# One level of Strassen's algorithm in the second half's output projection of an attention layer

## The chip, the core and the metric

The kernel runs on one core of a Trainium2 chip. TensorE (PE in the profile) multiplies matrices into the accumulator memory PSUM, VectorE (DVE), ScalarE (ACT) and GpSimd (POOL) do elementwise work, and SyncE (SP) issues the transfers between the chip's main memory and the working memory SBUF. Every engine works through its own queue in order. The metric is the device time of one execution in microseconds.

## The reference, cut

One layer of a decoder: a sliding-window attention with a sink, a gate, and one output projection between two RMS norms. SEQ is 1024, D_MODEL and BRANCH are 2048, all in float32.

```python
def reference(x, g_pre, g_post, w_in_a, w_out_a, sinks_a, ...):
    h = rmsnorm(x, g_pre[0])
    o, z = swa_sink_mixer(h, w_in_a[0], sinks_a[0])     # q, k, v, z = split(h @ w_in)
    y = (o.astype(z.dtype) * jax.nn.silu(z)) @ w_out_a[0]
    return x + rmsnorm(y, g_post[0])
```

What the change concerns is the last product, u @ w_out with u = o * silu(z): 1024 tokens by 2048 by 2048.

## The kernel before

The 1024 tokens are worked in two halves of 512, four blocks of 128 each. A half goes through v and k, then eight quads of heads (the input projection's q and z columns with attention between them, `in_phase`), then the output projection. Attention of the last quad's blocks is still running when the output projection begins; the constants `SPILL`, `TSL_LAST` and `VSL_LAST` place it among the first 13 k steps.

Products are computed to float32 accuracy in three passes: both factors are split in a high part `hi` (rounded by ACT) and a low part `lo` (the rest, subtracted on DVE), and hi·hi, lo·hi and hi·lo are added in PSUM. `passes` names the three pairs; `k` steps of 128 are the contraction.

Weights come through `stream`, a list of granules of 128x512 in the order of use. `next_granule` takes the next, and keeps the splitting `LOOK_W` = 3 granules and the loads `LOOK_DMA` = 5 ahead. In the first half `pump_split` stores each low part to memory (`kept`), and in the second half it is loaded back, so that DVE subtracts no weights there. The activations' parts come through `parts`: `next_part` keeps the splits of u (`u_hi`, `u_lo`, lines 562 and 563) two ahead.

The second half's output projection runs over four chunks of 512 output columns. For chunks 0 to 2, `out_slot` takes one weight granule and one part of u for each of 16 k steps and issues 12 matmuls, three passes for four token blocks, into four PSUM banks; `y_evac` squares and scales them. Chunk 3's weights (`wl_hi`, `wl_lo`) are loaded meanwhile into the room of h1, and chunk 3 is done block by block (line 843): when a block's 48 matmuls are over, its norm is known, and its four pieces are scaled, added to x and stored (lines 850 to 859) while PE works on the next block.

The program's order on each engine is set by the framework's scheduler from the order of the code, except where `keep_in_program_order` pins it.

Of the kernel before, what the change touches and what calls it, by code (L numbers as in the profile page):

```python
# [46 lines left out]
LOOK_DMA = 5  # L47
WARM = 8
# [16 lines left out]
def tile_swa_layer(  # L65
# [93 lines left out]

    stream = []  # L160
    for half in range(2):
# [9 lines left out]
        for c in range(3 if half else 4):  # L171
            for k in range(KC):
                stream.append((src_out(c, k), 1, "out", ("out", c, k)))
                if half and c and k % 2:
                    kl = 8 * (c - 1) + k // 2
                    stream.append((src_out(3, kl), 1, kl, ("out", 3, kl)))
# [3 lines left out]
    wl = []  # L180
# [5 lines left out]
    def pump_dma(limit):  # L186
        while state["dma"] < min(limit, len(stream)):
            i = state["dma"]
            src, nk, kind, key = stream[i]
            raw = gp.tile([P, 512], F32, tag="raw", name="raw")  # L190
            nc.sync.dma_start(raw.rearrange("p (k c) -> p k c", k=nk) if nk > 1 else raw, src)
            lo = None
            if key in kept:
                lo = wl[1][:, kind, :] if isinstance(kind, int) else lo_tile()
                nc.sync.dma_start(lo.bitcast(F32), kept[key])
# [3 lines left out]
    def pump_split(limit):  # L199
        while state["split"] < min(limit, len(stream)):  # L200
            i = state["split"]
            pump_dma(i + 1)
            raw, lo = raws.pop(i)
            kind, key = stream[i][2:]
            if isinstance(kind, int):
                hi = wl[0][:, kind, :]
            else:
                hi = gp.tile([P, 512], F32R, tag="g_hi", name="g_hi", bufs=G_BUFS)
            nc.scalar.copy(hi, raw)  # L209
            if lo is None:  # L210
                lo = lo_tile()
                eng = nc.gpsimd if kind == "in" and key[2] == 1 else nc.vector
                eng.tensor_tensor(lo, raw, hi.bitcast(F32), op=ALU.subtract)  # L213
                kept[key] = dram.tile([P, 512], F32, name=f"lo{i}")
                nc.sync.dma_start(kept[key], lo.bitcast(F32))
# [3 lines left out]
    def next_granule(look_split=LOOK_W, look_dma=LOOK_DMA):  # L219
        while isinstance(stream[state["use"]][2], int):  # L220
            state["use"] += 1
# [10 lines left out]
    def x_transpose(xs, k, h):  # L232
        pt = ps.tile([P, NB, P], F32, tag="o" if k % 4 == 3 else "s", name="pt_x", bufs=O_BUFS if k % 4 == 3 else S_BUFS)
        for b in range(NB):
            nc.tensor.transpose(pt[:, b, :], xs[:, b, :], ident)
        pt = pt.rearrange("p b t -> p (b t)")
        nc.scalar.activation(h[0][:, k, :], pt, AF.Copy, scale=gcol[:, k : k + 1])
        nc.vector.scalar_tensor_tensor(
            h[1][:, k, :], pt, gcol[:, k : k + 1], h[0][:, k, :].bitcast(F32), op0=ALU.mult, op1=ALU.subtract
# [41 lines left out]
    def v_diff(pool, kv):  # L281
        y = pool.tile([P, 2, NB, P], F32R, tag="vy", name="v_y", bufs=1)
        d = pool.tile([P, NB, P], F32, tag="vd", name="v_d", bufs=1)
# [38 lines left out]
    def in_slot(acc, h, g, fresh, done):  # L322
        gr = next_granule()
        for i in range(4):
            k = g * 4 + i
            for j, (w, hh) in enumerate(passes(gr, h)):
# [3 lines left out]
                    rhs=hh[:, k, :],  # L330
# [185 lines left out]
    def in_phase(half, h, u, pool):  # L516
# [3 lines left out]
        for i in range(NQUAD):  # L520
# [3 lines left out]
            if i % 2 == 0:  # L524
                y = {}
                at(s0 + VSL[half] - 3, lambda y=y, kv=i // 2: y.update(t=v_diff(pool, kv)))
# [86 lines left out]
    def v_slot(pvs, h, k, gr):  # L613
        i = k % 2
        for b in range(NB):
            for j, (w, hh) in enumerate(passes(gr, h)):
                mm = nc.tensor.matmul(  # L617
                    pvs[b // 2][:, b % 2, :],
                    lhsT=hh[:, k, b * P : (b + 1) * P],
# [9 lines left out]
    h_hi = hp.tile([P, KC, HALF], F32R, tag="hh", name="h_hi0")  # L629
    h_lo = hp.tile([P, KC, HALF], F32R, tag="hl", name="h_lo0")  # L630
    h0 = (h_hi, h_lo)
# [74 lines left out]
    rrow1 = const.tile([P, HALF], F32, name="rrow1")  # L706
    with tc.tile_pool(name="att0", bufs=1) as att:
# [19 lines left out]
    h1 = (  # L727
        hp.tile([P, KC, HALF], F32R, tag="hh", name="h_hi1"),
        hp.tile([P, KC, HALF], F32R, tag="hl", name="h_lo1"),
    )  # L730
    with tc.tile_pool(name="out0", bufs=1) as op:
# [14 lines left out]
        def chunk_split(k):  # L746
# [3 lines left out]
            nc.scalar.activation(h1[0][:, k, :], xt, AF.Copy, scale=gcol[:, k : k + 1])  # L750
            nc.vector.scalar_tensor_tensor(
                h1[1][:, k, :], xt, gcol[:, k : k + 1], h1[0][:, k, :].bitcast(F32), op0=ALU.mult, op1=ALU.subtract
# [32 lines left out]
    parts += [lambda k=k: (u1[:, k, :], 512) for c in range(3) for k in range(KC)]  # L785
    parts += [lambda b=b, j=j: (u1[:, 4 * j : 4 * j + 4, b * P : (b + 1) * P], P) for b in range(NB) for j in range(4)]
    with tc.tile_pool(name="att1", bufs=1) as att:
# [12 lines left out]
        accs = out_accs(0)  # L800
        for k in range(SPILL):
            run_events(128 + k)
            out_slot(accs, k, k == 0, False)
# [4 lines left out]
    wl += (  # L808
        hp.tile([P, KC, 512], F32R, tag="hh", name="wl_hi"),
        hp.tile([P, KC, 512], F32R, tag="hl", name="wl_lo"),  # L810
    )
    with tc.tile_pool(name="out1", bufs=1) as op:
        junk = op.tile([P, 512], BF16, name="junk2")
        for c in range(3):
            if c:
                accs = out_accs(c)
            gpo = op.tile([P, 512], F32, tag="gpo", name="gpo1", bufs=2)
            broadcast_row(gpo, g_post[:, c * 512 : (c + 1) * 512])
            for k in range(SPILL if c == 0 else 0, KC):
                out_slot(accs, k, k == 0, k == KC - 1)  # L820
                run_events(128 + 16 * c + k)
            for b in range(NB):
                y_evac(accs[b], 1, b, c, yts[b][:, c * 512 : (c + 1) * 512], gpo, junk)
        pump_split(len(stream))
        assert not events, sorted(events)
        gpo = op.tile([P, 512], F32, tag="gpo", name="gpo1", bufs=2)
        broadcast_row(gpo, g_post[:, 3 * 512 : 4 * 512])
        part = op.tile([P, NB], F32, name="part")
        nc.vector.tensor_reduce(part, ssp[:, 1, :, 0:3], axis=AX.X, op=ALU.add)
        nc.vector.tensor_scalar(part, part, 1.0 / D, EPS, op0=ALU.mult, op1=ALU.add)  # L830
        for b in range(NB):
            blk = NB + b
            acc = ps.tile([P, 512], F32, tag="acc", name="acc_l", bufs=4)
            xt = []
            for c in range(4):
                xt.append(op.tile([P, 512], F32, tag="xt1", name="xt1", bufs=4))
                nc.sync.dma_start(xt[c], xf[blk * P : (blk + 1) * P, c * 512 : (c + 1) * 512])
            for k in range(KC):
# [41 lines left out]
```

## Time and profile before

| | |
|---|---|
| median of 3 runs | 1275.54 us (1273.07 to 1280.38) |
| the profiled execution | 1278.27 us, its span 1276.6 us |
| PE busy | 1247.0 us (98%), granted clock 0.992 on average |
| DVE, ACT, POOL busy | 830.6, 783.2, 337.1 us |
| moved by DMA | 274 MB, 215 GB/s on average |
| second half's output projection | first matmul at 1084.9 us, end of the last at 1268.1 us |

Times within the profile are us from the start of the span. Busy time of PE counts matmuls that overlap, so PE's rate is read from the distance of starts. A group's row gives its count, busy time, mean ns of one, and the engine's idle time before its instructions with what ended it.

### The profile page before, as it was taken

To read this page: it belongs to the slowest core of one execution; us is meant where nothing else is said; L and a number is where in the kernel's file an instruction comes from. 1 tells how busy PE (TensorE), PEld (TensorE's weight loads), DVE (VectorE), ACT (ScalarE), POOL (GpSimd) and SP (SyncE) were. 2 spreads that over 40 slices of the span, in tenths; PEclk is the share of its full clock that TensorE was granted. 3 is DMA by queue.
4 is the path that set the end of the run, shared out by engine and by line. 5 is a ranking of instruction groups with operands and counts; after the bars stand their busy time and mean duration, and the time that the engine had idled before them with its cause. 6 is when DMAs were issued, how large, how long until landed. Compare 5 with 4: busy or idle time off the path is not lost.

```text
span 1276.6 us, 20454 instructions
## 1 busy us (share of the span) xinstructions
PE 1247.0 (98%) x5889; PEld 1043.8 (82%) x5889; DVE 830.6 (65%) x2365; ACT 783.2 (61%) x2087; POOL 337.1 (26%) x549
## 2 busy tenths in 40 slices
PE   8989999999999989999999999999999999999997
PEld 8878888888887877888898888888888888877785
DVE  5636767667676688677732278787787777832344
ACT  4526767666666677555533377777767767854531
POOL 1332536536535532000003022242232232200000
PEclk9989999999999999999999999999999999999999
DMA  8556777767676755899886667667767676876625
GB/s 289 157 181 205 224 225 228 221 217 237 215 233 210 232 159 168 230 271 252 253 265 194 190 208 209 210 205 208 213 202 218 191 226 183 290 257 229 226 70 182
DMA packets 302576, 274.03 MB, mean 215 GB/s; under 512 B 51568, under 2 KB 213888, under 8 KB 302464
## 3 DMA queue, kind: packets, MB, share of 16 engines
q1 hardware_dynamic: 302464, 272.73, 70.0%
q8 instruction: 47, 0.77, 0.2%
q14 instruction: 65, 0.53, 0.2%
HBM read 198.21 MB, written 74.45 MB: 214 GB/s over the span
## 4 chain that ended last, share of the span: by engine, by line
PE 54%; DMA 3%; ACT 1%; issue 1%; DVE 1%; POOL 0%; DVEq 0%; POOLq 0%; ACTq 0%; SPq 0%
PE acc_i L318 28%; PE acc_o L318 10%; PE acc_s L318 7%; DMA raw<-in_w_out_a 3%; PE acc_l L843 3%; PE o_ps L447 2%; PE acc_v L617 2%; PE acc_k L318 2%; PE s_ps L318 1%; ACT u_hi L562 1%; ACT g_hi L209 0%; DVE y L855 0%; ACT junk L587 0%; DVE u_lo L563 0%; ACT wl_hi L209 0%
## 5 line engine op out<-in xcount | busy, mean ns | idle before, releaser
L318 PE MATMUL acc_i<-h_hi,g_hi 128*128 128x512 f32 x1024 | 401.3, 392 | 2.0 <-ACT g_hi L209 2.0
L318 PE MATMUL acc_i<-h_hi,g_lo 128*128 128x512 f32 x1024 | 401.0, 392 | 1.7 <-DVE g_lo L213 1.7
L318 PE MATMUL acc_i<-h_lo,g_hi 128*128 128x512 f32 x1024 | 400.7, 391 | 0.0
L209 ACT CAST g_hi<-raw 128x512 fp32r<-128x512 f32 x400 | 245.7, 614 | 123.8 <-PE acc_i L318 49.5
L318 PEld LDWEIGHTS acc_i<-h_hi,g_hi 128*128 128x128 f32 x1024 | 192.8, 188 | 41.2 <-ACT g_hi L209 2.4
L318 PEld LDWEIGHTS acc_i<-h_lo,g_hi 128*128 128x128 f32 x1024 | 193.0, 188 | 40.0
L318 PEld LDWEIGHTS acc_i<-h_hi,g_lo 128*128 128x128 f32 x1024 | 193.0, 189 | 34.0 <-DVE g_lo L213 2.0
L213 DVE TENSOR_TENSOR g_lo<-raw,g_hi 128x512 fp32r<-128x512 f32 x176 | 127.4, 724 | 62.0 <-ACT g_hi L209 60.0
L374 ACT ACTIVATE t<-t,m 128x129 f32<-128x129 f32 x256 | 102.6, 401 | 95.7 <-DVE m L364 93.9
L563 DVE TENSOR_TENSOR u_lo<-u,u_hi 128x512 fp32r<-128x512 f32 x128 | 88.9, 697 | 111.0 <-ACT u_hi L562 104.9
L425 POOL TENSOR_SCALAR_AFFINE_SELECT g<-f 64x512 fp32r<-64x512 f32 x112 | 99.8, 892 | 171.1 <-ACT f L421 135.3
L562 ACT CAST u_hi<-u 128x512 fp32r<-128x512 f32 x128 | 78.9, 618 | 84.9 <-PE acc_o L318 29.0
L405 ACT COPY px<-wt 32x128 f32<-32x128 f32 x324 | 96.3, 297 | 28.6 <-DVE wt L399 25.0
L318 PE MATMUL acc_o<-g_hi,u_hi 128*128 128x512 f32 x256 | 101.9, 398 | 4.6 <-DVE z L510 3.6
L318 PE MATMUL acc_o<-g_lo,u_hi 128*128 128x512 f32 x256 | 101.1, 395 | 0.0
L318 PE MATMUL acc_o<-g_hi,u_lo 128*128 128x512 f32 x256 | 100.5, 398 | 0.1
L364 DVE CUSTOM_DVE_ANT_0 t<-s_ps,t,nsink 128x128 f32<-128x128 f32 x256 | 87.9, 348 | 5.2
L345 POOL COPY t<-nsink 128x4 f32<-128x4 f32 x64 | 12.8, 203 | 277.4 <-DVE w L385 132.8
L144 POOL TENSOR_TENSOR rs_r<-rs_v,mhalf 128x1 f32<-128x1 f32 (+1 forms) x10 | 6.3, 645 | 297.0 <-DVE rs_v L142 297.0
L318 PE MATMUL s_ps<-k_x,q 128*128 128x320 f32 x256 | 76.6, 310 | 3.5 <-POOL q L503 3.5
L362 DVE COPY_PREDICATED s_ps<-mask,s_ps 128x64 f32<-128x64 uint32 x224 | 49.0, 223 | 46.0 <-PE s_ps L318 44.6
L422 DVE TENSOR_TENSOR f<-px,f 128x512 fp32r<-128x512 f32 x64 | 50.7, 793 | 41.6 <-ACT f L421 41.2
(150 smaller groups left out, 2179.3 us busy)
## 6 DMA issues: line engine op xcount, KB each, us to landing
raw<-in_w_in_a SPq DMA_DIRECT2D x288, 256.0 KB, 3.6
lo<-g_lo SPq DMA_DIRECT2D x208, 256.0 KB, 2.7
g_lo<-lo SPq DMA_DIRECT2D x192, 256.0 KB, 3.5
raw<-in_w_out_a SPq DMA_DIRECT2D x128, 256.0 KB, 4.0
pd<-wt SPq DMA_DIRECT2D x28, 256.0 KB, 2.2
px<-pd SPq DMA_DIRECT2D x112, 64.0 KB, 2.2
xp<-in_x SPq DMA_DIRECT2D x16, 256.0 KB, 3.9
xb<-in_x SPq DMA_DIRECT2D x64, 64.0 KB, 4.1
```

The source lines that it names most:

```text
L209: nc.scalar.copy(hi, raw)
L213: eng.tensor_tensor(lo, raw, hi.bitcast(F32), op=ALU.subtract)
L318: ins = nc.tensor.matmul(*args, **kw)
L362: nc.vector.copy_predicated(s3[:, :, P:], mask.unsqueeze(1).broadcast_to([P, 2, QTR]), s3[:, :, 0:QTR])
L364: nc.vector.tensor_tensor_reduce(out=t[:, 0:P], in0=s3[:, 0, QTR:], in1=t[:, 0:P], scale=1.0, scalar=nsink[:, i : i + 1], op0=ALU.add, op1 ...
L374: nc.scalar.activation(t, t, AF.Exp, bias=m, scale=-1.0, accum_out=den)
L405: copy(x[qrows[3 - k], c, :], wt[qrows[c], 3 - k, :])
L422: pin(nc.vector.tensor_tensor(f[:, 1], x, f[:, 0].bitcast(F32), op=ALU.subtract))
L425: nc.gpsimd.affine_select(out=g[dst].rearrange("p a (s i) -> p (a s) i", i=HD), in_=f[HD:P, l].rearrange("p a (s i) -> p (a s) i", i=HD).b ...
L562: nc.scalar.copy(hi_v, src)
L563: nc.vector.tensor_tensor(lo_v, src, hi_v.bitcast(F32), op=ALU.subtract)
L843: nc.tensor.matmul(acc, lhsT=uu[:, i * P : (i + 1) * P], rhs=w[:, k, :], start=k == 0 and j == 0, stop=k == KC - 1 and j == 2,)
```

## The change

The second half's product is cut in halves: tokens in two (256 each), k in two (1024 each), and output columns in pairs of chunks (c and c + 1, for c = 0 and 2). For each pair, seven products of halves take the place of eight (Winograd's form with shared sums). With u's quarters u(t, k) and the weights' quarters v, y, z, x (`w_form`, 8 granules each, loaded by `form_loads` into the room of h1):

- products 1 and 2 take plain weights, 3 the plain quarter z; 7 takes z - y, 6 the sum x + (z - y), 4 takes v less that sum, 5 takes z - x. These sums are made in place, 64 in all, on POOL.
- on the side of u, products 5, 6, 7 and 3 take sums of quarters, made on DVE (`u_part`, `u_last`; lines 854, 858, 860 and 869).
- `FORMS` gives the order of the 28 steps of a pair. A step (`form_step`) takes one part of u (two k of 256 tokens) and two weight granules, and issues 12 matmuls, 6 for each granule, into two PSUM banks; steps are counted by n from 0, and step 28 begins the second pair.
- products are added up afterwards: `s1_copy` and `s5_copy` on ACT, `c11`, `c2` and `c12` on DVE, with the squares on ACT (line 971) and the product by the gain on POOL or DVE (line 972).
- the sums' low parts are subtracted on DVE when used (line 201), as are plain weights whose low part isn't stored any more: the first half now stores low parts of chunk 2 and of the second half of k in chunks 1 and 3 only.
- the last product of the second pair is done for token block 0 and then 1 (`lasts`), 48 matmuls; the four blocks are finished by `finish` (line 1014) around it.

To make room, h is held in halves (`new_h`), `rrow1` is the tile `rrow`, and `v_diff` uses the scratch tile `tmp` in the second half.

```diff
+W_TAGS = (("hlo0", "v"), ("hhi0", "y"), ("hhi1", "z"), ("hlo1", "x"))
+FORMS = [(prod, i) for prod, n in ((1, (0, 4)), (2, (0, 3)), (7, (0, 4)), (4, (0, 3)), (2, (3, 4)), (4, (3, 4)),
+                                   (5, (0, 4)), (6, (0, 4)), (3, (0, 4))) for i in range(*n)]
...
+    def form(c, prod, j):
+        if prod == 1:
+            return src_out(c, j), 1, "out", ("out", c, j)
+        key = {2: ("out", c, 8 + j), 3: ("out", c + 1, 8 + j)}.get(prod)
+        def load():
+            x, y, z, v = (w_form[n][:, j, :] for n in "xyzv")
+            if prod == 7:
+                nc.gpsimd.tensor_tensor(y, z, y, op=ALU.subtract)
+            elif prod == 4:
+                nc.gpsimd.tensor_tensor(v, v, x, op=ALU.subtract)
+            elif prod == 5:
+                nc.gpsimd.tensor_tensor(y, z, x, op=ALU.subtract)
+            if key not in kept:
+                return None
...
+            nc.sync.dma_start(lo.bitcast(F32), kept[key])
+            return lo
+        def split(lo):
+            src = w_form[{7: "y", 5: "y", 2: "v", 4: "v", 6: "x", 3: "z"}[prod]][:, j, :]
...
+            nc.scalar.copy(hi, src)
+            if lo is None:
+                lo = lo_tile()
+                nc.vector.tensor_tensor(lo, src, hi.bitcast(F32), op=ALU.subtract)
+            return hi, lo
...
-                kept[key] = dram.tile([P, 512], F32, name=f"lo{i}")
-                nc.sync.dma_start(kept[key], lo.bitcast(F32))
+                if kind != "out" or key[1] == 2 or key[1] % 2 and key[2] >= 8:
+                    kept[key] = dram.tile([P, 512], F32, name=f"lo{i}")
+                    nc.sync.dma_start(kept[key], lo.bitcast(F32))
...
+    def form_loads(n):
+        def load(name, k, c, jp):
+            for j in (2 * jp, 2 * jp + 1):
+                nc.sync.dma_start(w_form[name][:, j, :], src_out(c, 8 * k + j))
+        c = 2 * (n // 28)
+        n %= 28
+        if n < 4:
+            load("v", 1, c, n)
+        if 2 <= n < 6:
+            load("y", 0, c + 1, n - 2)
+            load("z", 1, c + 1, n - 2)
+        if 6 <= n < 10:
+            load("x", 0, c, n - 6)
+        if 7 <= n < 11:
+            for j in (2 * n - 14, 2 * n - 13):
+                x, y = (w_form[m][:, j, :] for m in "xy")
+                nc.gpsimd.tensor_tensor(x, y, x, op=ALU.add)
...
+    def form_step(n):
+        prod, i = FORMS[n % 28]
...
+        u = next_part()
+        for j in range(2):
+            gr = next_granule()
+            for b in range(2):
+                for q, (w, uu) in enumerate(passes(gr, u)):
+                    c0 = j * 2 * P + b * P
+                    ins = nc.tensor.matmul(
+                        accs[b], lhsT=uu[:, c0 : c0 + P], rhs=w,
+                        start=prod != 3 and i + j + q == 0, stop=i == 3 and j == 1 and q == 2, skip_group_check=True,
+                    )
...
+        def c2(c):
+            for b in range(2):
+                nc.vector.tensor_tensor(s1[:, b, :], s1[:, b, :], bank["c"][b], op=ALU.add)
+                nc.vector.tensor_tensor(mid[:, b, :], s1[:, b, :], bank["a"][b], op=ALU.add)
+            for b in range(2):
+                ct = sum_tile()
+                nc.vector.tensor_tensor(ct, mid[:, b, :], bank["d"][b], op=ALU.add)
+                y_take(ct, 2 + b, c, nc.gpsimd)
...
+        def c12(b, c):
+            ct = sum_tile()
+            nc.vector.tensor_tensor(ct, s1[:, b, :], bank["b"][b], op=ALU.add)
+            y_take(ct, b, c + 1, nc.vector)
...
+        lasts = [next_granule() for _ in range(8)]
+        for b in range(2):
...
+            if b == 0:
+                part_sum(slice(2, 4))
+                finish(2, xt2)
+                xt3 = x_load(3, xt_tiles())
+                finish(3, xt3)
+            c12(b, 2)
+            finish(b, xt1 if b else xt0)
```

What this does to the order of the engines is shown at three places. On DVE, after the last attention block, in the first chunk of the output projection before:

```order
L463 TENSOR_TENSOR u_8188<-s_o,z 128x128 x2
L563 TENSOR_TENSOR u_lo<-u_8188,u_hi 128x512 x4
L588 TENSOR_TENSOR y_13579<-acc_o,gpo_13588 128x512 x2
L588 TENSOR_TENSOR y_13580<-acc_o,gpo_13588 128x512
L563 TENSOR_TENSOR u_lo<-u_8188,u_hi 128x512
```

and, on DVE, around products 2, 4 and 5 of the first pair now (w_v, w_y are weight sums, u_sum the sums of u, c_t an output sum):

```order
L515 TENSOR_TENSOR u_8127<-s_o,z 128x128 x2
L201 TENSOR_TENSOR g_lo<-w_v,g_hi 128x512
L858 TENSOR_TENSOR u_sum<-u_8127 128x512 x4
L615 TENSOR_TENSOR u_lo<-u_8127,u_hi 128x512
L201 TENSOR_TENSOR g_lo<-w_v,g_hi 128x512 x2
L615 TENSOR_TENSOR u_lo<-u_sum,u_hi 128x512
L977 TENSOR_TENSOR c_t<-s_8128,acc_f 128x512
L860 TENSOR_TENSOR u_sum<-u_sum,u_8127 128x512
```

Where a step had one u_lo, it now has one u_lo, up to two g_lo and often a sum. On POOL, at the end of attention, before (g are attention's masked weights, px its transposed pieces, rs_r the norm's scale):

```order
L405 COPY px<-wt 32x128 x3
L425 AFFINE_SELECT g<-f 64x512 x2
L405 COPY px<-wt 32x128 x3
L425 AFFINE_SELECT g<-f 64x512 x2
L144 TENSOR_TENSOR rs_r<-rs_v,mhalf 128x1 x4
```

and on POOL now, from the middle of the first pair's weight sums:

```order
L177 TENSOR_TENSOR w_v<-w_v,w_x 128x512
L179 TENSOR_TENSOR w_y<-w_z,w_x 128x512 x3
L477 AFFINE_SELECT g<-f 64x512
L177 TENSOR_TENSOR w_v<-w_v,w_x 128x512
L179 TENSOR_TENSOR w_y<-w_z,w_x 128x512
L177 TENSOR_TENSOR w_v<-w_v,w_x 128x512
L477 AFFINE_SELECT g<-f 64x512
```

Attention's last POOL work stands between weight sums, and each sum waits for what it reads and overwrites. Last, the end of DVE's queue before, where block 3 alone is left (acc_l is the last matmul's bank):

```order
L563 TENSOR_TENSOR u_lo<-u_8188,u_hi 128x512
L142 TENSOR_SCALAR rs_v<-ssp,part 128x1
L852 TENSOR_TENSOR y_13581<-acc_l,gpo_14434 128x512
L146 SCALAR_TENSOR_TENSOR rs_w<-rs_r 128x1
L147 TENSOR_TENSOR rs_w<-rs_w,rs_v 128x1
L148 SCALAR_TENSOR_TENSOR r_114<-rs_w,rs_r 128x1
L855 SCALAR_TENSOR_TENSOR y_13581<-y_13581,r_114,xt_14713 128x512
```

and on DVE now, from the sum of the last bank (the row L998) on:

```order
L998 TENSOR_TENSOR c_t<-s_8128,acc_f 128x512
L145 TENSOR_SCALAR rs_v<-ssp,part 128x1 x3
L972 TENSOR_TENSOR y_13618<-c_t,gpo_14128 128x512
L145 TENSOR_SCALAR rs_v<-ssp,part 128x1
L149 SCALAR_TENSOR_TENSOR rs_w<-rs_r 128x1 x2
L150 TENSOR_TENSOR rs_w<-rs_w,rs_v 128x1 x2
L151 SCALAR_TENSOR_TENSOR r_114<-rs_w,rs_r 128x1 x2
L149 SCALAR_TENSOR_TENSOR rs_w<-rs_r 128x1
L1014 SCALAR_TENSOR_TENSOR y_13619<-y_13619,r_114,xt_14539 128x512
L1014 SCALAR_TENSOR_TENSOR y_13619<-y_13619,r_114,xt_14540 128x512
```

All sixteen operations of line 1014, those of the blocks that were complete earlier too, now stand behind the sum of the last bank.

More of the change, by code (lines that the diff above doesn't have):

```diff
@@ L202, in pump_split @@
             pump_dma(i + 1)
-            raw, lo = raws.pop(i)
[L204 to L208, printed above, removed]
+            kind, key = stream[i][2:]
+            if kind == "form":
+                splits[i] = stream[i][1](raws.pop(i))
+                state["split"] += 1
+                continue
+            raw, lo = raws.pop(i)
+            hi = gp.tile([P, 512], F32R, tag="g_hi", name="g_hi", bufs=G_BUFS)
             nc.scalar.copy(hi, raw)
```

226 lines of the change are left out of this document (156 added, 70 removed).

## The prediction

> **What bounds the kernel now.** I read the engine lines of the page first, then the whole kernel cut into the stretches of its last stage, then that stage's groups and waits, and last the final microseconds in order of time.
>
> ```profile
> PE 1247.0 (98%) x5889; PEld 1043.8 (82%) x5889; DVE 830.6 (65%) x2365; ACT 783.2 (61%) x2087; POOL 337.1 (26%) x549
> ```
>
> PE bounds the kernel as a whole. What this change is worth must be read from the stage that it rewrites: the second half's output projection, from its first matmul at 1084.9 us to its last one's end at 1268.1 us, and the tail behind it.
>
> ```profile
> 1084.89 0.39 PE L318 MATMUL acc_o<-g_hi,u_hi 128*128 128x512 f32 x1
> ...
> 1262.28 0.39 PE L843 MATMUL acc_l<-wl_hi,u_lo 128*128 128x512 f32 x1
> ...
> 1267.71 0.39 PE L843 MATMUL acc_l<-wl_hi,u_lo 128*128 128x512 f32 x1
> ```
>
> Start to start counts, since matmuls overlap. Between the last two rows lie 24 intervals: 5.43 / 24 = 0.226 us a matmul. The stage's 768 matmuls are 173.8 us at that rate and the stage is 183.2 us long; attention's last matmuls and small gaps make the other 9. So PE is the limit here too, and the other engines have room:
>
> ```profile
> 1084.90:1126.00 41.10, 41.10 (x197) 34.55 (x196) 30.46 (x95) 31.90 (x85) 8.43 (x16) 1.00 0.82 279
> 1126.00:1268.10 142.10, 140.38 (x606) 111.99 (x604) 53.62 (x91) 62.12 (x126) 1.65 (x3) 1.00 0.58 193
> ...
> DVE u_lo L563 <- ACT u_hi L562: 77.1, 41, 6.3
> ```
>
> Columns are PE, weight loads, DVE, ACT, POOL, granted clock, DMA share, GB/s. While attention's last blocks run (first row) DVE is 74% busy and ACT 78%. After that DVE is at 38% and POOL is empty: DVE waits 77 us in total for ACT's high parts, with little to do. That idle room is what the change spends.
>
> **The removal.** 12 matmuls make one step, and 52 steps plus 48 matmuls in the end are 672, against 768. 96 x 0.226 = 21.7 us less of PE, which is the largest gain possible.
>
> **What is added to DVE and POOL.** Before, a weight tile served 12 matmuls and its low part came ready from memory. Now a tile of weights or of weight sums serves 6, and 72 tiles have the low part subtracted on DVE again, besides 5 plain ones. The prices come from the groups of operations of this stage (the third row, POOL's, from those of the whole kernel); columns are the count, busy us and mean ns, then idle time before:
>
> ```profile
> L563 DVE TENSOR_TENSOR u_lo<-u,u_hi 128x512 fp32r<-128x512 f32 x61 | 42.3, 697 | 80.9 <-ACT u_hi L562 77.1 <-PE acc_o L318 3.6
> L588 DVE TENSOR_TENSOR y<-acc_o,gpo 128x512 f32<-128x512 f32 x8 | 5.5, 691 | 4.8 <-DMA xt<-in_x 4.1 <-ACT junk L587 0.6
> L213 POOL TENSOR_TENSOR g_lo<-raw,g_hi 128x512 fp32r<-128x512 f32 x32 | 41.5, 1298 | 29.9 <-ACT g_hi L209 14.4 <-DMA raw<-in_w_in_a 12.2 <-DMA lo<-g_lo 2.0
> L209 ACT CAST g_hi<-raw 128x512 fp32r<-128x512 f32 x45 | 27.7, 617 | 1.8 <-PE acc_o L318 1.8
> ...
> 1084.90:1126.00 41.10, 8.41 (x12) 1.00 0.82 279
> ...
> L209 ACT CAST g_hi<-raw 128x512 fp32r<-128x512 f32 x14 | 8.6, 616 | 1.8 <-PE acc_o L318 1.8
> L562 ACT CAST u_hi<-u 128x512 fp32r<-128x512 f32 x13 | 7.9, 615 | 2.4 <-DVE u L463 1.3 <-PE acc_o L318 0.9
> ```
>
> A full-width DVE operation (128x512) is 0.69 us, one on POOL with two inputs 1.29 to 1.30. The last three rows are of 1084.9 to 1126 alone: the u_lo work and ACT's casts in it. So attention's own work in this stage is 30.5 - 8.4 = 22 us on DVE, and 31.9 - 8.6 - 7.9 = 15 us on ACT. Now stage by stage, PE against DVE, counted in the changed order.
>
> A, steps 0 to 23 of the first column pair (all products but the third). PE: 288 x 0.226 = 65, and 5 for attention's matmuls: 70 us. DVE: 45 weight splits, 22 splits of u, 17 sums of u: 84 x 0.69 = 58; two sums from PSUM 1.4; attention 22: 81 us. DVE alone is 11 us longer than PE, and a lookahead of three weight tiles (4 us of PE) can't carry that. So in A DVE sets the pace, even if nothing disturbs it. ACT (45 + 22 casts of 0.62, 15 of attention, 4 of copies and squares) is 61 us and stays under it.
>
> B, steps 24 to 34, whose low parts come from memory. PE: 132 x 0.226 = 30 us; DVE: 26 full-width operations, 18 us. The SP queue issues some 39 transfers of 0.26 MB there; at the 319 GB/s of the row below these are 32 us.
>
> ```profile
> 1084.90:1112.00 27.10, 27.10 (x133) 22.83 (x132) 23.68 (x79) 22.50 (x63) 5.40 (x12) 1.00 0.93 319
> ```
>
> C, steps 35 to 51. PE: 204 x 0.226 = 46 us. DVE: 32 weight splits, 19 of u, sums worth 11, 2 from PSUM: 64 x 0.69 = 44 us. Level.
>
> D, the last 48 matmuls: 11 us.
>
> **POOL against DVE.** 64 weight sums go to POOL, with 10 products by the gain: 34 in A, some 20 in B, some 18 in C. POOL is no bound by itself (34 x 1.29 = 44 us in A), but look at one collision, DVE and POOL in order of time:
>
> ```profile
> 317.26 0.89 DVE L513 SCALAR_TENSOR_TENSOR z<-th,z 128x512 f32<-128x512 f32 x1
> 318.07 0.28 DVE L363 SCALAR_TENSOR_TENSOR t<-distb,s_ps 128x128 f32<-128x128 f32 x1
> 318.27 1.58 DVE L213 TENSOR_TENSOR g_lo<-raw,g_hi 128x512 fp32r<-128x512 f32 x1
> ...
> 317.69 1.62 POOL L284 TENSOR_TENSOR v_d<-v_n 128x512 f32<-128x512 f32 x1
> ...
> 89.06 0.69 DVE L213 TENSOR_TENSOR g_lo<-raw,g_hi 128x512 fp32r<-128x512 f32 x1 [4.73 <-ACT g_hi L209]
> ```
>
> A split that takes 0.69 us alone took 1.58 us: it ended 0.54 us after POOL's operation had ended (319.31), as if it had stood still before. POOL's was itself 0.33 us longer than its 1.29, behind the DVE operation before. The one with an input in PSUM (L363) kept its pace. In the Trainium skill, "SBUF — State Buffer", section "Who interferes with whom", this is a lock: a DVE instruction with two SBUF inputs and a GpSimd instruction that reads SBUF exclude each other for their whole length. The trace agrees (0.69 against 1.58 us), and the rule speaks against this change, since splits and sums of u and the weight sums are all of that kind; by it with 1.29 us lost for each of the 34, A alone would be some 125 us.
>
> The price of one POOL operation to a DVE that is the bound lies between 0 (it falls beside work from PSUM, or in a pause) and 1.15 us (1.29 less the 0.14 that overlapped at the end). I take the row's own loss, 1.58 - 0.69 = 0.89, times the share of DVE's time that has two SBUF inputs: in A (58 + about 8 of attention's 22) / 81 = 0.8, so 0.7 us each; in C nearly all, 0.86. A: 81 + 34 x 0.7 = 105 us. B: 18 + 20 x 0.7 = 32, beside PE's 30 and the transfers' 32: 32 us. C: 44 + 18 x 0.86 = 60, less the 4 of lookahead: 56 us. D: 11. The sum is 204 us against 183.2: 21 us longer. Bounds: with 0 it is 81 + 30 + 46 + 11 = 168 (15 shorter); with 1.15 it is 120 + 34 + 65 + 11 = 230 (47 longer).
>
> **The tail.** Before, three of the four token blocks are finished and stored while PE works on the next; only the last stands behind the last matmul:
>
> ```profile
> 1268.20 0.60 ACT L850 ACTIVATE junk<-acc_l 128x512 bf16<-128x512 f32 x1 [7.82 <-PE acc_l L843]
> 1269.05 0.68 DVE L852 TENSOR_TENSOR y<-acc_l,gpo 128x512 f32<-128x512 f32 x1
> 1270.38 2.74 DVE L855 SCALAR_TENSOR_TENSOR y<-y,r,xt 128x512 f32<-128x512 f32 x4
> ...
> xt<-in_x SPq DMA_DIRECT2D x16, 256.0 KB, 4.6
> out<-y SPq DMA_DIRECT2D x16, 256.0 KB, 3.9
> ```
>
> That is 8.5 us, to the span's end at 1276.6. In the changed order all 16 final operations stand on DVE behind the sum c_t that waits for the last matmul: c_t and a product (1.4), the scales (some 16 small ones of 0.16 to 0.21, 2.8), 16 x 0.685 = 11.0, half a microsecond for block 3's x, whose buffers are block 2's, and 3.9 for the last store: about 20 us. The 20 transfers from the first store on need 16 us at 319 GB/s and end no earlier. Tail: +11.5 us, nothing covers it, and I know of no row that could make it less than +9 or more than +14.
>
> Sum: +21 + 11.5 = +32. The profiled execution took 1278.27 us, 1.7 more than its span and 2.7 more than the median of the runs, 1275.54; a difference carries over, so I forecast 1275.5 + 32.5 = 1308 us.
>
> Costed at nothing: the first half stores 32 low parts less, but PE didn't wait there; the scratch tile that the value difference now shares with tanh is read out before ACT's tanh comes up; the row of scales reuses a tile whose readers are done; the weight loads at the start (8 + 32 transfers) wait for h1's buffers and then take 33 us, under A's 105. If A came out at PE's 70, these and POOL's sums would be late next.
>
> **The rivals.** First, PE stays the bound: DVE catches up by running ahead and POOL's sums fall beside work from PSUM. Then the stage is 152 + 5 = 157 us, the tail 20, and the time 1275.5 - 26 + 11.5 = 1261. For it: the 77 us that DVE idles today. Against it: A needs 81 us of DVE in 70, and the idle is after attention's end, not there; it decides below about 74 us in A. Chance 0.08.
>
> Second, DVE paces A but the collisions cost almost nothing, since POOL's operations find gaps: 168 + 20, so 1275.5 - 15 + 11.5 = 1272, no measurable change (0.5%, 6.4 us, is what a measurement can tell here). For it: many of today's collisions are short, as DVE comes late in POOL's operation:
>
> ```profile
> 160.52 0.99 DVE L213 TENSOR_TENSOR g_lo<-raw,g_hi 128x512 fp32r<-128x512 f32 x1 [0.39 <-ACT g_hi L209]
> ...
> 159.67 1.30 POOL L213 TENSOR_TENSOR g_lo<-raw,g_hi 128x512 fp32r<-128x512 f32 x1 [1.29 <-ACT g_hi L209]
> ```
>
> Here 0.30 us were lost. Against it: that was an engine with pauses (POOL is 26% busy on the page); in A, POOL would be over 40% busy, and a DVE without pauses meets each of its operations. Chance 0.16.
>
> Third, worse: PE, which now waits in every step, loses its clock.
>
> ```profile
> 500.00:505.00 5.00, 2.83 (x12) 1.88 (x10) 4.14 (x8) 4.24 (x11) 0.74 (x1) 1.00 0.46 127
> 505.00:510.00 5.00, 4.26 (x12) 3.38 (x13) 2.09 (x6) 1.15 (x3) 1.05 (x1) 0.51 0.61 206
> ```
>
> After a stretch in which PE was busy 2.8 of 5 us the clock was granted at half. A step is then 5.4 us and not 2.7, more than the 4.4 us that DVE needs in A; if half of the 41 steps of A and C ran so, 20 x about 1.5 = 30 us come on top: 1338. In the Trainium skill, "TensorE: Matmul & The Clock Gate", Part 1, halving needs an idle window of about 3.4 us. A's waits, some 1.7 us a step, would be too short, if spread. Chance 0.12.
>
> That the change removes no matmuls is excluded: its order holds 96 fewer of this stage.
>
> **How the numbers follow.** The forecast has 0.64: 1308, in its own range 1284 (half of the 0.7) to 1336 (the full 1.15 with the tail). The range 1268 to 1338 takes in the second rival and part of the third, and leaves out the first. Faster by over 0.5%: the first rival and a quarter of the second, 0.12; within 0.5%: the rest of the second, 0.12; slower: 0.76.
>
> **What the profile would show.** Right: DVE over 90% busy in steps 0 to 23 and again near the end, PE gaps there released by DVE's g_lo; g_lo's mean above 0.9 us; POOL's w_y, w_x and w_v sums above 1.29; over 15 us from last matmul to end, with 16 final operations of 0.69 in a row. Wrong: g_lo at 0.70 while POOL is busy (second rival), or PE without gaps until the last product (first); a granted clock below 0.9 in the stage speaks for the third.

## The result and the profile after

The changed kernel takes 1329.08 us (median of 4 runs, 1324.74 to 1334.54), the kernel before, run beside it, 1274.3 us (1272.56 to 1280.38). The ratio is 1.0423, with a 95% interval of 1.0367 to 1.0479: slower, by some 55 us. The forecast was 1308 us, in a range up to 1338.

Below, stages A to D and the tail are those of the prediction. Their ends are counted in the trace from the stage's 672 matmuls, 12 to a step. First the stretches of the changed kernel: A, B, C, D, tail. Columns are PE, weight loads, DVE, ACT, POOL, granted clock, DMA share, GB/s.

```profile
1083.10:1199.00 115.90, 85.62 (x322) 65.64 (x321) 108.35 (x172) 61.00 (x136) 59.95 (x50) 0.81 0.44 153
1199.00:1234.30 35.30, 32.50 (x134) 25.68 (x133) 31.90 (x27) 23.33 (x47) 32.06 (x20) 0.95 0.71 253
1234.30:1294.90 60.60, 49.47 (x206) 37.40 (x205) 53.73 (x61) 33.37 (x62) 30.33 (x19) 1.00 0.21 72
1294.90:1305.90 11.00, 11.00 (x49) 8.79 (x47) 8.56 (x12) 4.15 (x10) 3.38 (x2) 1.00 0.09 34
1305.90:1329.70 23.80, 0.01 (x1) 0.00 (x0) 15.33 (x39) 1.45 (x4) 2.72 (x4) 0.56 0.63 220
```

The stage is 222.8 us long where it was 183.2, the tail 23.8 where it was 8.5: 54.9 us in all. It began 1.8 us earlier, which leaves the 53.1 us between the two spans (1329.7 and 1276.6). In A, DVE is busy 108 of 116 us: it sets the pace, and PE, whose busy time there still holds overlaps, doesn't. PE's largest wait in the stage is for DVE's splits of the weights (us in total, times, longest):

```profile
PE acc_f L918 <- DVE g_lo L201: 22.9, 14, 5.4
```

The loss isn't spread evenly. Here are two short stretches (step 7, and steps 35 to 39), and between them one without POOL's work (steps 16 to 23); same columns:

```profile
1117.40:1140.00 22.60, 7.59 (x20) 4.96 (x19) 22.50 (x30) 5.80 (x14) 22.29 (x16) 0.58 0.00 0
...
1175.20:1199.20 24.00, 23.51 (x97) 19.01 (x96) 21.33 (x34) 14.89 (x26) 0.28 (x1) 0.93 0.65 212
...
1234.20:1260.80 26.60, 16.08 (x60) 10.38 (x59) 26.60 (x18) 8.50 (x15) 24.61 (x15) 1.00 0.03 10
```

In the first and the last, DVE and POOL are both busy all the time and PE stands. In the last, 18 DVE operations take 26.6 us, 1.48 each. In the middle one POOL is empty, 34 DVE operations take 21.3 us, and all of its eight steps but the first take PE's own 2.72 us. The groups of the stage show the same by tiles (count, busy us, mean ns of one, idle before):

```profile
L201 DVE TENSOR_TENSOR g_lo<-w_y,g_hi 128x512 fp32r<-128x512 f32 x32 | 37.0, 1167 | 0.1
L615 DVE TENSOR_TENSOR u_lo<-u,u_hi 128x512 fp32r<-128x512 f32 x21 | 29.0, 1396 | 1.3 <-ACT u_hi L614 1.3
L201 DVE TENSOR_TENSOR g_lo<-w_x,g_hi 128x512 fp32r<-128x512 f32 x16 | 10.7, 686 | 0.8 <-ACT g_hi L198 0.8
L437 DVE TENSOR_TENSOR w<-t,rec 128x192 f32<-128x192 f32 (+2 forms) x9 | 8.1, 925 | 0.0
L457 DVE COPY px<-wt 32x128 f32<-32x128 f32 x12 | 7.2, 598 | 0.2
L515 DVE TENSOR_TENSOR u<-s_o,z 128x128 f32<-128x128 f32 x8 | 6.0, 787 | 0.1
...
L179 POOL TENSOR_TENSOR w_y<-w_z,w_x 128x512 f32<-128x512 f32 x16 | 26.5, 1677 | 4.5 <-DVE g_lo L201 4.3
```

The split of w_x, when POOL has nothing to do, is 0.686 us; the same operation on w_y, beside POOL's sums, is 1.167 us. POOL's last sums take 1.68 us instead of 1.29 to 1.30. The last three DVE rows are attention's own work. In order of time the two engines take turns (start, length):

```profile
1125.53 1.31 POOL L177 TENSOR_TENSOR w_v<-w_v,w_x 128x512 f32<-128x512 f32 x1
1125.64 1.75 DVE L201 TENSOR_TENSOR g_lo<-w_y,g_hi 128x512 fp32r<-128x512 f32 x1
1126.81 1.72 POOL L179 TENSOR_TENSOR w_y<-w_z,w_x 128x512 f32<-128x512 f32 x1
```

The split ends 0.55 us after POOL's first sum, and POOL's second 1.14 us after the split.

The tail, PE's last matmul first and then DVE in order of time, and one row of the chain of waits (the second fence):

```profile
1305.52 0.39 PE L1046 MATMUL acc_f<-w_hi,u_lo 128*128 128x512 f32 x1
...
1303.85 1.78 DVE L972 TENSOR_TENSOR y<-c_t,gpo 128x512 f32<-128x512 f32 x1
1305.55 0.68 DVE L998 TENSOR_TENSOR c_t<-s,acc_f 128x512 f32<-128x512 f32 x1
...
1307.49 0.67 DVE L998 TENSOR_TENSOR c_t<-s,acc_f 128x512 f32<-128x512 f32 x1
...
1319.12 0.75 DVE L1014 SCALAR_TENSOR_TENSOR y<-y,r,xt 128x512 f32<-128x512 f32 x1 [1.94 <-DMA xt<-in_x]
1319.79 2.73 DVE L1014 SCALAR_TENSOR_TENSOR y<-y,r,w_x 128x512 f32<-128x512 f32 x4
```
```profile
1313.30 5.80 DMA xt<-in_x
```

The last matmul ends at 1305.9, but the sum that needs it starts at 1307.49: DVE was late, behind products that had met POOL's (1.78 us instead of 0.68). Then DVE stands 1.94 us for block 3's x, whose transfer is 5.80 us of the chain.

### The profile page after: what moved, and what is told of

Same layout as the page of the kernel before. It is cut to its first block, busy times and chain, and to the rows that moved or that the text cites. A ratio compares the mean times of both kernels' runs of the same rounds, so it can differ in the third digit from the quotient of the medians.

```text
span 1329.7 us, 20452 instructions
## 1 busy us (share of the span) xinstructions
PE 1243.7 (94%) x5793; PEld 1034.3 (78%) x5793; DVE 962.1 (72%) x2483; ACT 811.0 (61%) x2135; POOL 454.3 (34%) x623
## 5 line engine op out<-in xcount | busy, mean ns | idle before, releaser
L259 ACT CAST g_hi<-raw 128x512 fp32r<-128x512 f32 x368 | 225.6, 614 | 115.3 <-PE acc_i L370 43.3
L263 DVE TENSOR_TENSOR g_lo<-raw,g_hi 128x512 fp32r<-128x512 f32 x184 | 132.4, 719 | 61.6 <-ACT g_hi L259 60.1
L457 ACT COPY px<-wt 32x128 f32<-32x128 f32 x324 | 96.3, 297 | 36.6 <-DVE wt L451 33.1
L918 PE MATMUL acc_f<-g_lo,u_hi 128*128 128x512 f32 x208 | 88.2, 427 | 27.8 <-DVE g_lo L201 22.9
L615 DVE TENSOR_TENSOR u_lo<-u,u_hi 128x512 fp32r<-128x512 f32 x88 | 75.3, 860 | 37.3 <-ACT u_hi L614 35.1
L614 ACT CAST u_hi<-u 128x512 fp32r<-128x512 f32 x88 | 54.4, 618 | 72.2 <-PE acc_s L370 33.7
L918 PE MATMUL acc_f<-g_hi,u_lo 128*128 128x512 f32 x208 | 85.9, 415 | 1.9 <-DVE u_lo L615 1.9
L918 PE MATMUL acc_f<-g_hi,u_hi 128*128 128x512 f32 x208 | 74.2, 417 | 6.2 <-ACT g_hi L259 3.8
L918 PEld LDWEIGHTS acc_f<-g_lo,u_hi 128*128 128x128 f32 x208 | 42.0, 202 | 45.1 <-DVE g_lo L201 31.3
L415 DVE SCALAR_TENSOR_TENSOR t<-distb,s_ps 128x128 f32<-128x128 f32 x256 | 71.4, 284 | 5.6
```

What stands on the lines that cost most here:

```text
L415: nc.vector.scalar_tensor_tensor(t[:, 0:P], distb, 2.0 ** -i, s3[:, 1, QTR:], op0=ALU.mult, op1=ALU.add)
L457: copy(x[qrows[3 - k], c, :], wt[qrows[c], 3 - k, :])
L614: nc.scalar.copy(hi_v, src)
L615: nc.vector.tensor_tensor(lo_v, src, hi_v.bitcast(F32), op=ALU.subtract)
L918: ins = nc.tensor.matmul(accs[b], lhsT=uu[:, c0 : c0 + P], rhs=w, start=prod != 3 and i + j + q == 0, stop=i == 3 and j == 1 and q == 2, s ...
```

## Experiments

The kernels ran in four groups besides the first pair, each with the kernel before on the same chip (its medians were 1270.57, 1271.35, 1273.56 and 1273.51 us). Ratios are to that. The stage's start in the profiled executions lay between 1076.0 and 1084.4 us; so stage lengths are compared rather than spans. A kernel whose sums are left out, or replaced by writes or copies, no longer computes the layer; it is there for its time alone.

| kernel | median us | ratio, 95% interval | A | B | C | tail |
|---|---|---|---|---|---|---|
| as changed | 1329.08 | 1.0423, 1.0367 to 1.0479 | 115.9 | 35.3 | 60.6 | 23.8 |
| no sums | 1277.65 | 1.0058, 1.0037 to 1.0079 | 82.6 | 32.0 | 47.4 | 23.0 |
| three writes for each sum | 1292.61 | 1.0176, 1.0152 to 1.0201 | 97.9 | 31.6 | 47.4 | 23.3 |
| the same, px copies on ACT | 1292.89 | 1.0152, 1.0121 to 1.0183 | 94.6 | 31.6 | 47.4 | 23.3 |
| one write for each sum | 1285.16 | 1.0099, 1.0070 to 1.0127 | 87.6 | 31.7 | 47.4 | 23.1 |
| one copy for each sum | 1296.13 | 1.0197, 1.0181 to 1.0212 | 93.8 | 30.8 | 54.1 | 23.6 |
| sums on DVE | 1311.56 | 1.0308, 1.0277 to 1.0339 | 105.0 | 35.1 | 51.0 | 23.6 |
| 16 more low parts kept | 1317.54 | 1.0369, 1.0344 to 1.0395 | 107.0 | 34.8 | 60.5 | 23.9 |
| no sums, low parts kept | 1273.76 | 1.0018, 1.0006 to 1.0031 | 79.0 | 31.7 | 47.4 | 23.9 |
| sums on DVE, low parts kept, tail mended | 1296.67 | 1.0211, 1.0189 to 1.0234 | 98.4 | 36.6 | 51.0 | 18.8 |
| no sums, low parts kept, tail mended | 1271.36 | 0.9983, 0.9966 to 1.0001 | 79.2 | 32.0 | 47.4 | 18.9 |

D was 11.0 us in every one.

**Without the sums.**

```diff
-                nc.gpsimd.tensor_tensor(y, z, y, op=ALU.subtract)
+                pass
...  the same for v - x, z - x and x + y
```

> Leaves out all 64 weight sums on POOL (the products then use plain weight tiles); splits, casts, matmuls, loads and the tail stay as they are. Theory (POOL's two-input sums and DVE's two-input operations exclude each other, and DVE paces the stage): g_lo back to about 0.70 us, steps 0 to 23 in 81 to 88 us instead of 116.1, steps 35 to 51 in 46 to 48 instead of 60.6, 24 to 34 in 31 instead of 35; 47 to 54 us less, 1275 to 1282 us. Rival 1 (the 40 loads at the start set the pace of steps 0 to 23): these steps stay above 105 us, about 1315. Rival 2 (PE's halved clock is a cause of its own and stays while PE waits for DVE at all): 20 to 30 us of the gain are missing, 1300 to 1310, with some 40 us at half clock left.

Measured: ratio 1.0058, A 82.6, B 32.0, C 47.4. The theory's numbers hold and both rivals fall. The stretches A and C of this kernel, and four of its groups:

```profile
1078.20:1160.80 82.60, 75.21 (x321) 60.84 (x320) 78.21 (x172) 60.25 (x136) 13.48 (x18) 0.94 0.61 214
...
1192.80:1240.20 47.40, 46.79 (x205) 38.10 (x204) 36.12 (x58) 33.64 (x62) 2.95 (x2) 1.00 0.29 98
```
```profile
L201 DVE TENSOR_TENSOR g_lo<-w_y,g_hi 128x512 fp32r<-128x512 f32 x32 | 22.7, 722 | 0.5 <-ACT g_hi L198 0.5
...
L437 DVE TENSOR_TENSOR w<-t,rec 128x192 f32<-128x192 f32 (+2 forms) x9 | 2.7, 325 | 0.0
L457 DVE COPY px<-wt 32x128 f32<-32x128 f32 x12 | 2.6, 220 | 0.2
L515 DVE TENSOR_TENSOR u<-s_o,z 128x128 f32<-128x128 f32 x8 | 2.0, 285 | 0.0
```

DVE's count of operations is the same in A (172), its busy time 30 us less. And yet this kernel, with 96 matmuls less and no sums to make, is still not faster than before: A stays near DVE's own 78 us, and the tail costs 14.5 us more than before.

**Writes in place of the sums.** Which part of POOL's work blocks DVE?

```diff
-                nc.gpsimd.tensor_tensor(y, z, y, op=ALU.subtract)
+                [nc.gpsimd.memset(y, 0.01) for _ in range(3)]
...  the same for v, y and x
```

> Each of the 64 weight sums on POOL is replaced by three writes of a constant to the same tile (no reading of SBUF), at some 0.5 us each, so POOL stays busy about 1.6 us for each as in the changed kernel, and the splits still wait for POOL's tile. Theory (it is POOL's reading beside DVE's two inputs that blocks): g_lo stays at about 0.70 us and the time is that of the kernel without sums plus at most 6 us, 1275 to 1288. Rival (POOL's tiles come late, or any POOL work on SBUF blocks DVE): g_lo above 1.0 us or long waits for POOL, 1315 to 1330.

Measured: 1292.61 us, between the two expectations, ratio 1.0176. C is as without sums, 47.4 us, with POOL at work; A is 97.9. Groups of this kernel:

```profile
L201 DVE TENSOR_TENSOR g_lo<-w_y,g_hi 128x512 fp32r<-128x512 f32 x32 | 22.3, 704 | 0.6 <-ACT g_hi L198 0.6
L457 DVE COPY px<-wt 32x128 f32<-32x128 f32 x12 | 17.1, 1427 | 0.2
...
L177 POOL MEMSET w_v<- 128x512 f32 x48 | 24.0, 524 | 15.3 <-ACT g_hi L198 14.2 <-DVE g_lo L201 0.7
```

The splits are back at 0.70 us, so it is the reading on POOL that holds up a two-input DVE operation, and writing doesn't. All 13 us that C lost are that. In the Trainium skill, "SBUF — State Buffer", section "Who interferes with whom", this is stated so: a DVE instruction with two SBUF inputs contends with a GpSimd instruction that reads SBUF, not with one that only writes; the trace agrees (1.167 against 0.704 us). But in A 15 us are left over no sums, and one DVE row grew far more than any other: the px copies (17.1 us against 2.6).

> The kernel that writes constants on POOL in place of the sums, with the attention's px copies (32x128, one SBUF input, four of each sixteen on DVE) moved from DVE to ACT in the second half. Theory (in the kernel with constants, steps 0 to 23 took 97.7 us and not 82 because DVE's px copies stood behind whole runs of POOL's writes: 17.1 us for 12 copies, 2.6 without POOL's work): steps 0 to 23 in 82 to 87 us, ratio to the kernel before 1.006 to 1.010. Rival (the 16 us are POOL's lateness with its tiles): no change, ratio 1.015 to 1.020.

```diff
-  copy = {"A": nc.scalar.copy, "P": nc.gpsimd.tensor_copy, "D": nc.vector.tensor_copy}[MOVES[n]]
+  copy = {"A": nc.scalar.copy, "P": nc.gpsimd.tensor_copy, "D": nc.scalar.copy if half else nc.vector.tensor_copy}[MOVES[n]]
```

Measured: A 94.6, ratio 1.0152, in an interval that overlaps that of the kernel it was made from. The theory fell: with the copies gone from DVE its busy time in A drops from 92 to 78 us, and A by 3. The copies now stand in ACT's queue, though, and PE waits for ACT's high parts, so this run doesn't show what A would be if they cost nothing anywhere:

```profile
PE acc_f L918 <- ACT g_hi L259: 5.7, 3, 5.2
PE acc_f L918 <- ACT g_hi L198: 4.8, 3, 4.1
```

So POOL's own time was tried, with `range(1)` in place of `range(3)`.

> As the kernel with three writes of a constant in place of each weight sum, with one write each: POOL is busy some 0.5 us for a sum's tile instead of 1.56, the waits between DMA, POOL, ACT and DVE are the same. Theory (with three writes, POOL's own length sets steps 0 to 23, 95 to 98 us: 34 tiles x 1.56 = 53 us beside attention's POOL work, in a window of some 50 us): with a third of it they fall to 82 to 86 us, ratio to the kernel before 1.005 to 1.009. Rival (the chain of waits through POOL costs this by itself, however short POOL's work): steps 0 to 23 stay above 92 us, ratio 1.013 or more.

Measured: A 87.6, ratio 1.0099. Between the two again: of the 15.3 us, 10.3 go when POOL's 1.56 us become 0.52, and 5.0 stay. The px copies on DVE shrink in the same run, from 17.1 us to 6.6 (12 of 0.55 us), so the two aren't separated here. That A fell by only 3 us when they left DVE speaks for POOL's length as the larger part. What the other 5 us are wasn't settled; the px copies, still 4 us above the 2.6 without the sums, may be part of it.

**A copy in place of each sum.**

```diff
-                nc.gpsimd.tensor_tensor(y, z, y, op=ALU.subtract)
+                nc.gpsimd.tensor_copy(y, z)
...  the same for v (from x), y (from z) and x (from y)
```

> Each of the 64 weight sums on POOL is replaced by a copy of one of its two inputs to the same tile (POOL reads one SBUF tile and writes one), some 1.1 us each. Theory (whatever reads SBUF on POOL excludes DVE's two-input operations): splits beside it are long again, g_lo of w_y above 1.0 us, 1305 to 1320, close to the changed kernel. Rival (only POOL's two-input operations exclude them; the kernel with writes alone showed that writing doesn't): g_lo at 0.70 us, 1278 to 1293.

Measured: 1296.13 us, between the two, ratio 1.0197. One collision and two groups:

```profile
1119.66 1.07 POOL L179 COPY w_y<-w_z 128x512 f32<-128x512 f32 x1
1120.18 1.09 DVE L201 TENSOR_TENSOR g_lo<-w_y,g_hi 128x512 fp32r<-128x512 f32 x1
1120.68 1.07 POOL L177 COPY w_v<-w_x 128x512 f32<-128x512 f32 x1
```
```profile
L201 DVE TENSOR_TENSOR g_lo<-w_y,g_hi 128x512 fp32r<-128x512 f32 x32 | 27.6, 877 | 0.7 <-ACT g_hi L198 0.7
...
L896 POOL COPY w_x<-w_y 128x512 f32<-128x512 f32 x16 | 11.2, 726 | 0.1
```

The split again ends 0.54 us after POOL's operation, as it does beside a sum. A copy that reads holds a split up in the same way. What was wrong is the size: a copy takes 0.73 us and not the 1.1 that I had put, so each takes less from DVE.

**The sums on DVE.**

```diff
-                nc.gpsimd.tensor_tensor(y, z, y, op=ALU.subtract)
+                nc.vector.tensor_tensor(y, z, y, op=ALU.subtract)
...  the same for v - x, z - x and x + y
```

> The 64 weight sums are computed on DVE instead of POOL; everything else is the same. Theory (full exclusion: a sum on POOL costs DVE 0.9 to 1.2 us, on DVE itself 0.69): steps 0 to 23 take 81 + 34 x 0.69 = 105 us instead of 116, steps 35 to 51 about 52 to 55 instead of 60.6; 15 to 23 us less, 1306 to 1314. Rival 1 (a sum on POOL costs DVE no more than 0.7, the price of the prediction): no change, 1325 to 1332. Rival 2 (the sums, in DVE's queue, hold up splits behind them while they wait for loads): over 1335.

Measured: A 105.0, C 51.0, and B unchanged at 35.1: the stage is 20.6 us shorter, the ratio 1.0308, 1.1 points below the changed kernel's. The theory's A came out, 105, though only 32 of the 34 operations counted there are sums (two are products by the gain, which stay on POOL): from the 82.6 measured without sums, 32 x 0.69 more are 104.7. C is a little below the expected 52 to 55, and neither rival came. A sum that the engine in need does itself costs A (105.0 - 82.6) / 32 = 0.70 us; one that another engine does "for free" costs it (115.9 - 82.6) / 32 = 1.04.

**More low parts from memory.**

```diff
-                if kind != "out" or key[1] == 2 or key[1] % 2 and key[2] >= 8:
+                if kind != "out" or key[1] % 2 == 0 or key[2] >= 8:
```

> The first half stores the low parts of 16 more weight tiles (products 1 and 2 of the first column pair), and the stage loads them instead of subtracting them again: 16 splits less on DVE in steps 0 to 23, 16 transfers of 0.26 MB more there. Theory (DVE paces these steps): 16 x 0.69 to 16 x 1.4 = 11 to 22 us less, steps 0 to 23 in 94 to 105 us, 1307 to 1318. Rival (the steps lost time lies in the POOL sums window, steps 3 to 15, or in the loads, not in products 1 and 2): under 5 us less, 1324 to 1330.

Measured: A 107.0, C unchanged at 60.5; the stage is 9.5 us shorter, a little less than the theory's low end of 11. The ratio is 1.0369, and its interval overlaps that of the changed kernel, so the gain is read from the stage.

> The kernel without the 64 weight sums, with the low parts of the first pair's products 1 and 2 also kept in memory, so 16 splits less in steps 0 to 23. Theory (what was left in these steps without the sums, 82 us against PE's 70, is DVE's own work): 82 - 16 x 0.69 = 71 us, PE the bound; stage 173 - 11 = 162, tail 23 as before it: 8 to 11 us less than without sums, a ratio to the kernel before of 0.997 to 1.000. Rival (loads at the start or ACT's casts set those 82 us; 16 more transfers come on top): no change, ratio 1.004 to 1.010.

Measured: A 79.0 and not 71, ratio 1.0018, between the two expectations. Most of A's gain didn't come, which speaks for the rival. A in three stretches (steps 0 to 2, 3 to 7, and 8 to 23), and a wait:

```profile
1080.40:1089.80 9.40, 9.40 (x46) 7.77 (x46) 8.11 (x29) 8.18 (x24) 1.49 (x4) 1.00 1.02 373
1089.80:1109.90 20.10, 18.17 (x78) 12.80 (x77) 17.47 (x47) 16.46 (x43) 3.56 (x7) 1.00 1.04 378
1109.90:1159.40 49.50, 45.49 (x201) 36.59 (x200) 47.89 (x84) 35.26 (x71) 6.83 (x7) 1.00 0.57 193
```
```profile
PE acc_f L918 <- DMA g_lo<-lo: 1.7, 6, 0.4
```

Through step 7 the DMA engines are full (share above 1, 373 to 378 GB/s). In steps 3 to 7 PE meets low parts that are just landing, and a step takes about 4 us. After that DVE is busy 47.9 of 49.5 us. So the loads seem to take over at the start, and DVE stays the limit behind it; no run separates the two.

**The best complete version, and the bound.** In the tail, block 3's x is loaded early, into tiles that are free by then, and the last pair's products go to DVE:

```diff
-                xt3 = x_load(3, xt_tiles())
...
         lasts = [next_granule() for _ in range(8)]
+        xt3 = x_load(3, [w_form["z"][:, c, :] for c in range(4)])
...
-                y_take(ct, 2 + b, c, nc.gpsimd)
+                y_take(ct, 2 + b, c, nc.vector if c else nc.gpsimd)
```

> The best complete version that the parts add up to: the sums on DVE, the 16 low parts kept, and in the tail block 3's x loaded early into the free tiles w_z instead of into block 2's, with the last pair's products by the gain on DVE. Steps 0 to 23: 105 - 16 x 0.69 = 94 us; the rest of the stage as with the sums on DVE (97 us), so 191; tail 23.6 - 1.9 (DVE's wait for x) - 1.2 to 1.7 (collisions with POOL's products) = 20 to 20.5. Ratio to the kernel before 1.018 to 1.022. Rival (tail bound by the stores and not by DVE): tail stays above 22.5, ratio above 1.021. Neither theory has it faster than before.

Measured: ratio 1.0211, tail 18.8 us, better than the 20 expected; A 98.4, above the 94, which wasn't followed further. That the ratio is the expected one is in part chance, since these two misses have opposite signs. Its tail in order of time: no wait is left in DVE's row of final operations.

```profile
1276.85 2.73 DVE L1014 SCALAR_TENSOR_TENSOR y<-y,r,xt 128x512 f32<-128x512 f32 x4
...
1279.92 2.74 DVE L1014 SCALAR_TENSOR_TENSOR y<-y,r,w_z 128x512 f32<-128x512 f32 x4
...
1282.76 5.39 DVE L1014 SCALAR_TENSOR_TENSOR y<-y,r,w_x 128x512 f32<-128x512 f32 x8
```

> What the scheme could reach at most here with this tail: no weight sums at all, the 16 low parts kept, block 3's x loaded early and the last pair's products on DVE. Stage as in the kernel without sums and with kept low parts (169 us), tail 19 instead of 23 to 24, as in the version with the sums on DVE: 4 to 5 us less, ratio to the kernel before 0.997 to 0.999, the same time within what can be measured. Rival (the tail's gain is lost again, since block 2 and 3's products now delay the last sums): ratio 1.001 or more.

Measured: 0.9983, interval 0.9966 to 1.0001, as expected. With its sums for nothing, the scheme would just meet the kernel before. No version here beats it by what can be measured.

**POOL's reading beside a DVE that has room.** The kernel before, with 64 two-input operations on POOL that nobody waits for, in chunks 1 and 2:

```diff
+                if c:
+                    for e in range(2):
+                        nc.gpsimd.tensor_tensor(dummy, u1[:, k, :], u1[:, 15 - k, :], op=ALU.subtract)
```

> The kernel before, with 64 subtractions of two SBUF tiles added on POOL at the start of its last stage's chunks 1 and 2; nothing reads their result. Theory (POOL's price is paid only where DVE is the bound): u_lo beside them goes from 0.70 to 1.3 to 1.7 us, DVE stays under 80% busy there, PE without gaps: within 0.3% of the kernel before. Rival (each collision reaches PE through the short lookahead): 64 x 0.3 to 64 x 0.9 = 19 to 58 us longer.

```profile
L563 DVE TENSOR_TENSOR u_lo<-u,u_hi 128x512 fp32r<-128x512 f32 x60 | 67.2, 1135 | 58.9 <-ACT u_hi L562 57.4 <-PE acc_o L318 1.3
...
L824 POOL TENSOR_TENSOR dummy<-u 128x512 f32<-128x512 f32 x64 | 94.7, 1480 | 11.6 <-PE acc_o L318 6.6
...
PE acc_o L318 <- DVE u_lo L563: 1.3, 3, 0.5
```

Measured: ratio 1.0012 (0.9994 to 1.0030). DVE's splits went from 697 to 1135 ns on average over the stage (1412 beside POOL's operations alone, within the expected 1.3 to 1.7 us), 25 us more in all. PE waited 1.3 us for them in the row shown and 0.4 in another. Collisions of the same kind cost nothing that could be measured where DVE had 59 us of idle left.

## Why the prediction was right, and where it was off

The measured 1329.08 us are 21 more than the forecast. A, B, C and the tail missed by 11, 3, 5 and 4 us, all to the same side; the stage's earlier start, 1.8 us, gives some of it back.

- **The bound moves to DVE; POOL's sums take from it.** Right, and shown: DVE is busy 108 of A's 116 us, g_lo is 1.167 us beside the sums, and taking the sums away brings 115.9 to 82.6. The end of the range worked out for no collisions, 81 us for A, was measured as 82.6, and 46 for C as 47.4.
- **A: 105 predicted, 115.9 measured. The price of one POOL operation, 0.7 us, was a little too small, and two terms were missing.** A loses 33.3 us to the sums (115.9 against 82.6). DVE's busy time grew by 30.1 of them (108.35 against 78.21), in the same 172 operations. The px copies, L457, are 4.6 of that (7.2 against 2.6); they have one SBUF input, and the prediction had counted such work as safe. The other 25.5 are operations with two SBUF inputs, 0.80 for each of the 32 sums, between the prediction's 0.7 and its row's full 0.89. In all that is close to the 24 us that its sum had for 34 operations. Attention's own rows are in it: L437 grew by 5.4 us and L515 by 4.0. The last 3.2 us are idle time of DVE, for which the sum had no term; and without the sums A was 82.6 us and not 81. So what failed is chiefly what the sum left out, the single-input copies and DVE's waits. Writes alone on POOL lengthen A too (87.6 us with one for each sum, 97.9 with three), which the prediction had not priced.
- **A sum of the range.** With 1.15 us an operation, B comes to 18 + 20 x 1.15 = 41 us and not to the 34 of the prediction, so that its upper bound for the stage is 237 us, 54 longer. The measured 222.8 lies below either.
- **B: 32 predicted, 35.3 measured.** Without the sums it was 32.0, and with them on DVE 35.1, so POOL's collisions alone don't explain these 3 us. Their cause stays open.
- **C: 56 predicted, 60.6 measured.** The sum took C as one stretch that DVE paces, 44 + 18 x 0.86 = 59.5, less 4 us for the lookahead. These 4 us are the step that failed. The collisions came in a heap, 15 of POOL's operations in steps 35 to 39, where PE ran dry, while all but one of the steps 40 to 51 ran at PE's pace and gave nothing back. That 59.5 comes so near is luck in part: DVE's own work in C is 36.1 us and not 44, and it is busy 53.7 of the 60.6. C loses 13.2 us to 47.4, and all of it goes when POOL only writes.
- **D: 11 us, as predicted.**
- **The tail: 20 predicted, 23.8 measured,** +15.3 where "not more than +14" had been said. The step that failed is the half microsecond for block 3's x: its transfer is 5.80 us of the chain, and DVE stood 1.94 us. Most of the rest is DVE's lateness at the last matmul, 1.6 us, from two operations that met POOL's products. With both mended it is 18.8, close to the terms without that half microsecond (19.1).
- **The first rival** (PE stays the bound) didn't come. **The second** (collisions cost nothing) didn't either; what it would have given can be read from the kernel without sums: 1.0058, not faster than before.
- **The third rival, the halved clock,** came in part: the prediction's sign for it, a granted clock below 0.9, is there in A (0.81).

```profile
1141.37 0.63 PE L918 MATMUL acc_f<-g_hi,u_hi 128*128 128x512 f32 x1
...
1145.17 0.40 PE L918 MATMUL acc_f<-g_hi,u_hi 128*128 128x512 f32 x1
```

  Matmuls recorded at 0.55 us or longer start 0.43 us apart instead of 0.226. There are 61 of them in the stage, at most 12.3 us more than at full clock, so it can't be the 30 us of that rival. With the sums on DVE there were still 36 such matmuls (7.2 us), and A came to what DVE's count alone gives. While DVE is busy without a pause, a slower PE costs nothing, so in A the clock's cost lies within DVE's idle time, 7.6 us there and 4.4 without sums. This speaks against a large cost of its own, but no run separates it. The prediction's argument against this rival, waits of some 1.7 us a step if spread, didn't hold: step 7 alone took 22.65 us.

## What to carry to other kernels

Work that is moved to an idle engine isn't free if its reads hold up the engine in need: here a sum on POOL cost the longest stretch 1.04 us, and on DVE itself 0.70. Before trading matmuls for elementwise work, count the second engine's time in the stage where it is fullest, and count the tail: a scheme that finishes all output blocks together moves their final operations behind the last matmul. And ask first what the bound would be if the new work cost nothing; here it was no gain (0.9983).

## What the runs showed of the hardware that was not expected

A DVE copy with a single SBUF input waits for POOL too, and at times for a whole run of its operations, even if these only write. In the kernel with three writes, DVE's rows and some of POOL's:

```profile
1104.47 6.86 DVE L457 COPY px<-wt 32x128 f32<-32x128 f32 x1
1104.67 0.52 POOL L896 MEMSET w_x<- 128x512 f32 x1
...
1110.74 0.51 POOL L177 MEMSET w_v<- 128x512 f32 x1
1111.36 0.23 DVE L414 COPY_PREDICATED s_ps<-mask,s_ps 128x64 f32<-128x64 uint32 x1
```

A copy of some 0.22 us takes 6.86 us, and ends when POOL's run of writes ends, while two-input splits beside such writes keep their 0.70 us. It isn't always a whole run: four such copies from 1088.32 us on took 2.08 us beside writes, each ending just after one write. In the Trainium skill, "SBUF — State Buffer", section "Who interferes with whom", copies can enter a mode that takes the port pair shared with GpSimd, and then wait for an instruction of it; the trace agrees that they wait (1427 ns on average against 220), and shows one waiting for many instructions on end. No run here shows which mode a copy was in.
